# A second write of zeroes to the output, just ahead of the first store of a weighted sum

## Chip, cores, metric

One core of a Trainium2 chip. The metric is the device time of one execution in microseconds (us), as the median of several runs.

## What is computed

For each of 16 x 1024 tokens there are two expert outputs of 512 numbers and two weights; the result is their weighted sum, all in float32.

```python
weights = combine_weights[..., np.newaxis]          # (16, 1024, 2, 1)
return np.sum(expert_outputs * weights, axis=2)     # (16, 1024, 2, 512) -> (16, 1024, 512)
```

That is 67 MB to read, 34 MB to write and little arithmetic per byte.

## The kernel before

The 16,384 tokens are spread over the 128 partitions of the on-chip memory, 128 tokens to each partition. A partition's 128 tokens are cut into ten tiles of 12 or 13 tokens (`TILES`). The first nine tiles cover the first 128 x 115 rows of the arrays (`main` = 115 tokens a partition, with consecutive tokens of one partition lying together), the last tile the remaining 128 x 13 rows.

One large buffer `et` has four rooms (`ROOM`, 13, 13, 12 and 13 tokens). Tile g goes into room g mod 4. A load (line 76, `load`) brings the two expert outputs of a tile's tokens into its room, up to 53,248 bytes a partition. All loads are issued from SyncE's queue. The first five loads (`FIRST`: 2, 11, 13, 12 and 13 tokens; the first two make up tile 0) fill the four rooms; every later load is issued after the store that frees its room, and waits for that store's landing.

The sums (`combine`) are made in place. For tiles 0 to 7 VectorE multiplies the whole tile by the weights in one instruction (line 88) and adds the two halves in another (line 97); the sums land in the front part of the room. In tile 8 ScalarE does a part of the products (line 92); in tile 9 ScalarE makes one product and VectorE a fused multiply-add token by token (lines 102 and 103).

The stores (line 130) are issued from ScalarE's queue for tiles 0 to 6 and from SyncE's queue for tiles 7 and 8 (one store) and 9. Both queues feed the same 16 DMA engines.

The order of the instructions on each engine is that of the code (`tc.manual_schedule()`); waits between engines are set by the framework from what is read and written. Each DMA signals its landing on one of eight semaphore lanes, and a DMA that takes a lane over waits until the lane's last holder has landed. An additional DMA therefore shifts the lanes of those that come after it.

Before anything else VectorE sets the small tile `zt` (16 partitions of 128 numbers) to zero (line 108), and ScalarE's queue writes it to the output (line 111): with the first 128 x 115 rows of the output seen as 16 equal stretches (`ahead`), the first 512 bytes of each stretch become zero. The stores later put the true values there. After it, the same queue loads the weights (line 79: one load of 920 bytes a partition; line 114: two of 104 bytes for 64 partitions each).

Of the kernel before, what the change touches and what calls it, by code (L numbers as in the profile page):

```python
# [1 line left out]

# [4 lines left out]


@with_exitstack
def kernel(  # L10
    ctx: ExitStack,
    tc: tile.TileContext,
    expert_outputs: bass.AP,
    combine_weights: bass.AP,
    out: bass.AP,
):

    nc = tc.nc
    b, s, k, h = expert_outputs.shape
    assert k == 2
    n = b * s
    P = nc.NUM_PARTITIONS
    per = n // P
    assert per * P == n

    ROOM = [13, 13, 12, 13]
    ROOMS = len(ROOM)  # L30
    SITE = [sum(ROOM[:i]) for i in range(ROOMS)]
    TILES = [13, 13, 12, 13, 13, 13, 12, 13, 13, 13]
    FIRST = [2, 11, 13, 12, 13]
    STORES = [[0], [1], [2], [3], [4], [5], [6], [7, 8], [9]]
    WHOLE = [0, 1, 2, 3, 4, 5, 6, 7]
    MIXED = [8]
    ALONE = 3
    FREE = {9: 0}
    LAST = 13
    assert all(c <= ROOM[g % ROOMS] for g, c in enumerate(TILES))  # L40
    assert sum(TILES) == per and [g for st in STORES for g in st] == list(range(len(TILES)))
    main = per - LAST
    starts = [sum(TILES[:g]) for g in range(len(TILES))]

    def rows(x):

        first = x[0 : P * main, :].rearrange("(p t) f -> p t f", p=P)
        second = x[P * main : n, :].rearrange("(p t) f -> p t f", p=P)
        return lambda t, c: first[:, t : t + c, :] if t < main else second[:, t - main : t - main + c, :]

    flat = out.rearrange("b s h -> (b s) h")
    eo = rows(expert_outputs.rearrange("b s k h -> (b s) (k h)"))
    cw = rows(combine_weights.rearrange("b s k -> (b s) k"))
    o = rows(flat)

    dt = mybir.dt.float32
    mult = mybir.AluOpType.mult
    add = mybir.AluOpType.add
    copy = mybir.ActivationFunctionType.Copy

    pool = ctx.enter_context(tc.tile_pool(name="all", bufs=1))
    et = pool.tile([P, sum(ROOM), k * h], dt)
    halves = et.rearrange("p j (k h) -> p (j k) h", k=k)
    wt = pool.tile([P, per * k], dt)
    wk = wt.rearrange("p (t k) -> p t k", k=k)
    zt = pool.tile([16, 128], dt)
    warm = pool.tile([P, 1], dt)

    def place(t):
        g = max(g for g in range(len(TILES)) if starts[g] <= t)  # L70
        return SITE[g % ROOMS] + t - starts[g]

    def load(t, c, **kw):
        at = place(t)
        assert place(t + c - 1) == at + c - 1
        nc.sync.dma_start(out=et[:, at : at + c], in_=eo(t, c), **kw)  # L76

    def weights(q, t, c):
        q.dma_start(out=wk[:, t : t + c, :], in_=cw(t, c))

    def combine(g, base):
        at, c, t0 = SITE[g % ROOMS], TILES[g], starts[g]
        if g in WHOLE or g in MIXED:
            room = halves[:, k * at : k * (at + c), :]
            x0, x1 = et[:, at : at + c, 0:h], et[:, at : at + c, h : 2 * h]
            if g in WHOLE:
                wb = wt[:, k * t0 : k * (t0 + c)].unsqueeze(2).to_broadcast([P, k * c, h])
                nc.vector.tensor_tensor(out=room, in0=room, in1=wb, op=mult)  # L88
            else:
                for i in range(ALONE, c):  # L90
                    x = et[:, at + i, 0:h]
                    nc.scalar.activation(out=x, in_=x, func=copy, scale=wt[:, k * (t0 + i) : k * (t0 + i) + 1])  # L92
                w1 = wk[:, t0 : t0 + c, 1:2].to_broadcast([P, c, h])
                nc.vector.tensor_tensor(out=x1, in0=x1, in1=w1, op=mult)  # L94
                w0 = wk[:, t0 : t0 + ALONE, 0:1].to_broadcast([P, ALONE, h])
                nc.vector.tensor_tensor(out=x0[:, 0:ALONE], in0=x0[:, 0:ALONE], in1=w0, op=mult)  # L96
            nc.vector.tensor_tensor(out=halves[:, base : base + c, :], in0=x0, in1=x1, op=add)  # L97
            return
        for i in range(c):
            t = k * (t0 + i)  # L100
            x0, x1 = halves[:, k * (at + i), :], halves[:, k * (at + i) + 1, :]
            nc.scalar.activation(out=x0, in_=x0, func=copy, scale=wt[:, t : t + 1])  # L102
            nc.vector.scalar_tensor_tensor(  # L103
                out=halves[:, base + i, :], in0=x1, scalar=wt[:, t + 1 : t + 2], in1=x0, op0=mult, op1=add
            )

    with tc.manual_schedule():
        nc.vector.memset(zt, 0.0)  # L108

        ahead = flat[0 : P * main, :].rearrange("(q t) h -> q (t h)", q=16)  # L110
        nc.scalar.dma_start(out=ahead[:, 0:128], in_=zt)  # L111
        weights(nc.scalar, 0, main)
        for half in (slice(0, P // 2), slice(P // 2, P)):
            nc.scalar.dma_start(out=wk[half, main:per, :], in_=cw(main, per - main)[half])
        nc.scalar.activation(out=warm, in_=nc.const_aps.tensor(1.0, (P, 1), dt), func=copy)  # L115

        t = 0
        for i, c in enumerate(FIRST):
            load(t, c, **({"max_dma_last_dim": k * h * 4} if i == 0 else {}))
            t += c  # L120
        assert t == sum(TILES[:ROOMS])
        for j, st in enumerate(STORES):
            room = FREE.get(st[0], st[0] % ROOMS)
            base, c = SITE[room] * k, 0
            for g in st:
                combine(g, base + c)
                c += TILES[g]
            assert c <= k * ROOM[room]
            q = nc.sync if j in (7, 8) else nc.scalar
            q.dma_start(out=o(starts[st[0]], c), in_=halves[:, base : base + c, :])  # L130
            for g in st:
                if g + ROOMS < len(TILES):
                    load(starts[g + ROOMS], TILES[g + ROOMS])


# [1 line left out]
_INS = ['expert_outputs', 'combine_weights']  # L137
_OUTS = [((16, 1024, 512), 'float32')]


# [23 lines left out]
```

## Time and profile before

| | |
|---|---|
| median of 3 runs | 238.86 us (238.84 to 238.99) |
| profiled execution, first to last instruction (span) | 237.1 us; the page gives no other time of it |
| bytes moved | 100.80 MB, on average 425 GB/s |
| VectorE busy | 190.0 us |
| ScalarE busy | 15.8 us |

In the profile's rows DVE is VectorE, ACT ScalarE, SP SyncE, POOL GpSimd; a trailing q (ACTq, SPq) is the sequencer of that engine, which issues the DMAs. q1 is the DMA queue fed by SyncE, q10 that fed by ScalarE. `et`, `wt` and `zt` are the buffers named above, `out_dram` the output. L97 is line 97 of the kernel. In rows of DMA queues there stand packets, MB, and the time that the packets took as a share of 16 engines over the stretch asked for; a packet is counted where it begins, so that a short stretch can show over 100%.

### The profile page before, as it was taken

What the parts mean: (1) busy time and instruction counts of PE and PEld (TensorE: products, weight loads), DVE (VectorE), ACT (ScalarE), POOL (GpSimd) and SP (SyncE); (2) the same over time, 40 slices, a digit from 0 to 9 for tenths busy, and PEclk for the clock granted to TensorE, in tenths of its full rate; (3) what the DMA queues carried; (4) which work ended last, traced back from release to release, by engine and by line L of the source; (5) the groups of instructions that cost most, each with busy time, mean ns of one, the idle gap of its engine ahead of it and who ended that gap; (6) DMA issues with size and microseconds to landing.
All of it is one profiled execution on the core that took longest, in us unless ns stands there. A gap on an engine that the chain in (4) does not pass through costs nothing.

```text
span 237.1 us, 154 instructions
## 1 busy us (share of the span) xinstructions
DVE 190.0 (80%) x33; ACT 15.8 (7%) x25; POOL 0.2 (0%) x4
## 2 busy tenths in 40 slices
DVE  0006999999999999999999998998499969919400
ACT  2000000000000000000000000000000055019200
POOL 0000000000000000000000000000000000000000
DMA  8999999989999999999899999999899999899996
GB/s 300 388 481 434 432 421 398 470 348 485 449 431 458 431 440 390 486 420 420 359 492 409 409 509 392 431 503 431 359 431 503 420 397 483 381 431 431 431 431 287
DMA packets 3344, 100.80 MB, mean 425 GB/s; under 512 B 512, under 2 KB 656, under 8 KB 912
## 3 DMA queue, kind: packets, MB, share of 16 engines
q1 hardware_dynamic: 2000, 77.33, 75.9%
q10 hardware_dynamic: 1344, 23.47, 23.0%
HBM read 67.24 MB, written 33.56 MB: 425 GB/s over the span
## 4 chain that ended last, share of the span: by engine, by line
DVE 55%; DMA 36%; issue 1%; ACT 0%; DVEq 0%; ACTq 0%; SPq 0%
DVE et L88 35%; DVE et L97 17%; DMA out_dram<-et 17%; DMA et<-in_expert_outputs_dram 12%; DMA wt<-in_combine_weights_dram 8%; DVE et L103 3%; ACT et L102 0%; DVEq L159 0%; ACTq L111 0%; DVE zt L108 0%; DVEq L88 0%; SPq L76 0%; ACTq L102 0%
## 5 line engine op out<-in xcount | busy, mean ns | idle before, releaser
L88 DVE TENSOR_TENSOR et<-et,wt 128x13312 f32<-128x13312 f32 (+1 forms) x8 | 110.0, 13754 | 23.8 <-DMA wt<-in_combine_weights_dram 18.7
L97 DVE TENSOR_TENSOR et<-et 128x6656 f32<-128x6656 f32 (+1 forms) x9 | 62.8, 6973 | 0.4
L92 ACT ACTIVATE et<-et,wt 128x512 f32<-128x512 f32 x10 | 6.2, 708 | 188.0 <-DMA et<-in_expert_outputs_dram 188.0
L103 DVE SCALAR_TENSOR_TENSOR et<-et,wt 128x512 f32<-128x512 f32 x13 | 8.7, 747 | 5.0 <-ACT et L102 5.0
L102 ACT ACTIVATE et<-et,wt 128x512 f32<-128x512 f32 x13 | 8.1, 707 | 14.0 <-DMA et<-in_expert_outputs_dram 14.0
L94 DVE TENSOR_TENSOR et<-et,wt 128x6656 f32<-128x6656 f32 x1 | 7.1, 7093 | 2.3 <-DMA et<-in_expert_outputs_dram 2.3
L96 DVE TENSOR_TENSOR et<-et,wt 128x1536 f32<-128x1536 f32 x1 | 1.8, 1751 | 0.0
L115 ACT ACT_TABLE_LOAD x1 | 1.3, 1283 | 3.1 <-issue 3.1
L108 DVE MEMSET zt<- 16x128 f32 x1 | 0.2, 165 | 0.8 <-PEq L148 0.8
L115 ACT ACTIVATE warm<-const-float32-1.0 128x1 f32<-128x1 f32 x1 | 0.2, 203 | 0.0
L148 POOL MEMSET const-bfloat16-1.0<- 128x1 bf16 x1 | 0.1, 102 | 0.0
L148 POOL MEMSET const-uint8-127<- 128x1 uint8 x1 | 0.1, 101 | 0.0
L148 POOL MEMSET const-float32-0.0<- 128x1 f32 x1 | 0.1, 99 | 0.2 <-issue 0.2
L148 POOL MEMSET const-float32-1.0<- 128x1 f32 x1 | 0.1, 98 | 0.0
## 6 DMA issues: line engine op xcount, KB each, us to landing
et<-in_expert_outputs_dram SPq DMA_DIRECT2D x7, 6656.0 KB, 32.2
out_dram<-et ACTq DMA_DIRECT2D x5, 3328.0 KB, 34.7
et<-in_expert_outputs_dram SPq DMA_DIRECT2D x2, 6144.0 KB, 41.1
out_dram<-et SPq DMA_DIRECT2D x1, 6656.0 KB, 19.9
out_dram<-et ACTq DMA_DIRECT2D x2, 3072.0 KB, 37.2
et<-in_expert_outputs_dram SPq DMA_DIRECT2D x1, 5632.0 KB, 18.2
out_dram<-et SPq DMA_DIRECT2D x1, 3328.0 KB, 14.0
et<-in_expert_outputs_dram SPq DMA_DIRECT2D x1, 1024.0 KB, 5.0
```

What stands on the lines that cost most here:

```text
L88: nc.vector.tensor_tensor(out=room, in0=room, in1=wb, op=mult)
L92: nc.scalar.activation(out=x, in_=x, func=copy, scale=wt[:, k * (t0 + i) : k * (t0 + i) + 1])
L94: nc.vector.tensor_tensor(out=x1, in0=x1, in1=w1, op=mult)
L96: nc.vector.tensor_tensor(out=x0[:, 0:ALONE], in0=x0[:, 0:ALONE], in1=w0, op=mult)
L97: nc.vector.tensor_tensor(out=halves[:, base : base + c, :], in0=x0, in1=x1, op=add)
L102: nc.scalar.activation(out=x0, in_=x0, func=copy, scale=wt[:, t : t + 1])
L103: nc.vector.scalar_tensor_tensor(out=halves[:, base + i, :], in0=x1, scalar=wt[:, t + 1 : t + 2], in1=x0, op0=mult, op1=add)
L108: nc.vector.memset(zt, 0.0)
L115: nc.scalar.activation(out=warm, in_=nc.const_aps.tensor(1.0, (P, 1), dt), func=copy)
L148: nc = _bacc.Bacc("TRN2", target_bir_lowering=False, num_devices=1)
```

## The change

The write of zeroes, memset and DMA, becomes a function `touch`. It is called where the write stood, and a second time in `combine`, behind the product of tile 0 and ahead of its sum. So the second memset stands on VectorE between these two instructions, and the second DMA on ScalarE's queue ahead of the store of tile 0, which covers the same rows and is made to wait for it. Line numbers move by five to eight.

```diff
+    ahead = flat[0 : P * main, :].rearrange("(q t) h -> q (t h)", q=16)
+
+    def touch():
+        nc.vector.memset(zt, 0.0)
+        nc.scalar.dma_start(out=ahead[:, 0:128], in_=zt)
+
     def combine(g, base):
...
                 nc.vector.tensor_tensor(out=room, in0=room, in1=wb, op=mult)
+                if g == 0:
+                    touch()
             else:
...
     with tc.manual_schedule():
-        nc.vector.memset(zt, 0.0)
-
-        ahead = flat[0 : P * main, :].rearrange("(q t) h -> q (t h)", q=16)
-        nc.scalar.dma_start(out=ahead[:, 0:128], in_=zt)
+        touch()
         weights(nc.scalar, 0, main)
```

## The prediction

> **What bounds the kernel now.** I read the page first, for who is busy and how evenly.
>
> ```profile
> DVE 190.0 (80%) x33; ACT 15.8 (7%) x25; POOL 0.2 (0%) x4
> ...
> DMA  8999999989999999999899999999899999899996
> DMA packets 3344, 100.80 MB, mean 425 GB/s; under 512 B 512, under 2 KB 656, under 8 KB 912
> ```
>
> VectorE works for 80% of the span, yet the row of DMA tenths holds an 8 or a 9 in every slice but the last. The 16 DMA engines are the suspect. A mean can hide a stage in which they wait, so I cut the span into stages (columns: stretch, its length, busy time of each engine, clock, DMA share, GB/s).
>
> ```profile
> 0.00:20.00 20.00, 0.44 (x2) 1.49 (x2) 0.20 (x4) 1.00 0.95 390
> 20.00:62.00 42.00, 41.93 (x5) 0.00 (x0) 0.00 (x0) 1.00 0.99 424
> 62.00:110.00 48.00, 47.93 (x5) 0.00 (x0) 0.00 (x0) 1.00 1.02 439
> 110.00:145.00 35.00, 34.52 (x4) 0.00 (x0) 0.00 (x0) 1.00 0.99 430
> 145.00:208.00 63.00, 55.91 (x7) 6.23 (x10) 0.00 (x0) 1.00 1.00 431
> 208.00:237.00 29.00, 9.29 (x14) 8.07 (x13) 0.00 (x0) 1.00 0.95 411
> ```
>
> The DMA share is 0.99 to 1.02 in every stage but the first and the last (a packet is counted where it begins, hence the 1.02). From 20 to 145 us VectorE is full as well; after 145 it has gaps (55.91 of 63 us). So two resources are full in the middle, and only one of them stays full to the end. Who sets the end is read from the chain of waits and from the last stores.
>
> ```profile
> 144.62 39.25 DMA out_dram<-et
> 183.92 28.80 DMA et<-in_expert_outputs_dram
> 213.56 8.04 DVE et L103 x12
> ```
>
> ```profile
> out_dram<-et SPq DMA_DIRECT2D x1, 6656.0 KB, 19.9
> out_dram<-et SPq DMA_DIRECT2D x1, 3328.0 KB, 14.0
> ```
>
> ```profile
> 208.61 0.35 SPq L130 DMA_DIRECT2D out_dram<-et  x1
> 222.29 0.34 SPq L130 DMA_DIRECT2D out_dram<-et  x1
> ```
>
> The chain runs through a store, the last load and the last sums, but look at what the queue does meanwhile. The store of tiles 7 and 8 is issued at 208.61 and lands 19.9 us later, at 228.5. The last store is issued at 222.29, 6.2 us before that, stands behind it on the same queue and lands at 236.3. The engines thus always have a store waiting; a delay of the last load or of the last sums by some us would be swallowed by these 6.2 us. What sets the end is the amount of work of the DMA engines, not the chain. A change moves the time only if it gives each engine more or less to do, makes a packet last longer, or leaves all queues empty for a while.
>
> **The change part by part.** The compiled program of the changed kernel shows one more memset on VectorE between the first product and the first sum, one more small DMA on ScalarE's queue ahead of store 0, and shifted semaphore lanes. In the timeline the place is this:
>
> ```profile
> 0.81 0.17 DVE L108 MEMSET zt<- 16x128 f32 x1 [0.81 <-PEq L148]
> 1.01 0.39 ACTq L111 DMA_DIRECT2D out_dram<-zt  x1
> 1.22 1.62 SPq L76 DMA_DIRECT2D et<-in_expert_outputs_dram  x3
> 1.43 0.45 ACTq L79 DMA_DIRECT2D wt<-in_combine_weights_dram  x1
> 4.92 0.33 SPq L76 DMA_DIRECT2D et<-in_expert_outputs_dram  x1
> 19.73 14.02 DVE L88 TENSOR_TENSOR et<-et,wt 128x13312 f32<-128x13312 f32 x1 [18.75 <-DMA wt<-in_combine_weights_dram]
> 33.78 7.09 DVE L97 TENSOR_TENSOR et<-et 128x6656 f32<-128x6656 f32 x1
> 40.79 14.02 DVE L88 TENSOR_TENSOR et<-et,wt 128x13312 f32<-128x13312 f32 x1
> 40.91 0.34 ACTq L130 DMA_DIRECT2D out_dram<-et  x1
> ```
>
> The memset costs 0.17 us by its first instance, with a handover of about 0.03 us (product end 33.75, sum start 33.78). VectorE has no gap from 19.73 to 145, so stores 0 to 5 are issued about 0.2 us later. That is not on the path that sets the end: the queues hold other work, and the last store has its 6.2 us. Cost at the end: 0; with the cover gone it would be 0.2 us. The memset also waits until the first write of zeroes has read `zt`. That and the landings of the first DMAs stand here (KB each, us from issue to landing):
>
> ```profile
> et<-in_expert_outputs_dram SPq DMA_DIRECT2D x1, 6656.0 KB, 33.5
> et<-in_expert_outputs_dram SPq DMA_DIRECT2D x1, 1024.0 KB, 5.0
> wt<-in_combine_weights_dram ACTq DMA_DIRECT2D x1, 115.0 KB, 18.2
> wt<-in_combine_weights_dram ACTq DMA_DIRECT2D x2, 6.5 KB, 31.0
> out_dram<-zt ACTq DMA_DIRECT2D x1, 8.0 KB, 3.9
> ```
>
> The first zeroes were issued at 1.0 and landed 3.9 us later, at 4.9, almost 29 us before the second memset: no wait.
>
> The DMA itself adds 16 packets of 512 bytes and 16 completion packets. Their price is in the stretch from 4 to 5 us, where the first zeroes went out:
>
> ```profile
> q1 hardware_dynamic: 100, 0.41, 98.4%
> q10 hardware_dynamic: 32, 0.01, 3.6%
> ```
>
> These 32 packets took 3.6% of 16 engines for 1 us, 0.58 us of engine time in all or 0.036 us of each engine. Cost at the end: +0.036 us, since the engines are full. [...]
>
> Store 0 must now wait for the zeroes to land, since both write the same rows. The zeroes can be issued at about 34.0 us, store 0 at 41.1: a cover of 7.1 us, the first sum. Near end: they land after 3.9 us, as the first did. Far end: store 0's own first packets began in the window from 45.6 to 46.2 us, 4.8 us after its issue; behind them one more load packet may come ahead of the completion. The size of such a packet is in the windows from 38 to 39 us and from 43.4 to 44.4 us (16 packets of the load of tile 2 each):
>
> ```profile
> q1 hardware_dynamic: 16, 0.79, 181.5%
> ```
>
> ```profile
> q1 hardware_dynamic: 16, 0.79, 220.2%
> ```
>
> ```profile
> q10 hardware_dynamic: 16, 0.43, 164.5%
> ```
>
> (The last row is store 0's first round, from 45.6 to 46.2.) One load packet takes 1.815 us of its engine. So the far end is 34.0 + 4.8 + 1.8 and some tenths to be noticed, 41 us: store 0 starts on time, or late by at most one packet, 1.8 us. Behind it on ScalarE's queue stands store 1, which is not ready until 62. Who waits for store 0 is load 5, into the room it frees:
>
> ```profile
> 67.80 0.33 SPq L76 DMA_DIRECT2D et<-in_expert_outputs_dram  x1
> ```
>
> ```profile
> et<-in_expert_outputs_dram SPq DMA_DIRECT2D x1, 6656.0 KB, 71.7
> ```
>
> Load 5 was issued at 67.80. The load ahead of it, the fifth, was issued at 4.9 and landed 71.7 us later, at 76.6. The load queue therefore had 8.8 us of work left, and 1.8 us of delay disappear in it. Cost: 0.
>
> The lanes: in the program of before the fifth load waits for the first zeroes' lane. With one DMA more, the fourth load waits for the first load (landed 5.0 us after its issue, so before 7) and the fifth for the weights (landed 18.2 us after an issue at 1.4, at 19.6). The third load, issued between 1.2 and 2.2, keeps the queue occupied until about 35 (33.5 us). Both are queued 15 us before their turn: cost 0. Later lanes pair with transfers that landed long before.
>
> The term whose size I cannot read is what the zeroes do to the **first store's stall**. The load packets from 43.4 took 220.2% of a 1 us window over 16 packets, 2.202 us each against 1.815: each engine lost 0.387 us once, as its first output packet came up. Two ends: the zeroes take that stall away (-0.387 us), or they bring another of the same size (+0.387 us). The nearest row is that of the first zeroes themselves: around them (4 to 5 us) 100 load packets took 157 ns each, so 16 small writes stalled nothing visible there, and their having gone out did not spare store 0 its stall 39 us later. I take 0 and keep both ends.
>
> Sum: 0 (VectorE) + 0.036 (packets) + 0 (landing) + 0 (lanes) + 0 (stall) = +0.04 us on the profiled execution's span of 237.1 us. The page gives no time beyond the span; the median of the runs, 238.86, is 1.8 us above it, which I take as unchanged. Forecast: 238.9 us.
>
> **The rivals.** What a measurement of this kernel can tell from no change I put at 0.2%, 0.48 us.
>
> *First-store stall gone.* The second touch comes 5 to 7 us before store 0 instead of 37, and what was lost in between is still there. 238.86 + 0.036 - 0.387 = 238.5. For it speaks that the stall occurs at the first store only; against it, that I only guess that closeness in time matters. Still inside 0.48 us.
>
> *Second stall.* The zeroes meet full queues and 16 engines that are moving 49 KB packets, and stop them as store 0 did, while store 0's stall remains: 238.86 + 0.036 + 0.387 = 239.3. Inside 0.48 us, barely.
>
> *Slower: the zeroes find the path cold.* The dearest such thing in the trace is the start. In the first 4 us:
>
> ```profile
> q1 hardware_dynamic: 145, 0.59, 53.5%
> ```
>
> That is 236 ns a packet (0.535 x 64 us / 145), against the 157 ns from 4 to 5 us: 145 x 79 ns over 16 engines, 0.72 us lost on each engine. If the zeroes, standing between load packets around 38 us, cost that much, the time is 238.86 + 0.036 + 0.72 = 239.6. It is decided by the loss of each engine: from 0.44 us up the result is slower. Against it: store 0, the same direction in larger packets, cost 0.387.
>
> *The landing counts in full.* Store 0 waits one load packet longer and nothing takes it up: 238.86 + 1.8 = 240.7, if the load queue ran dry before load 5. Against it stand the 8.8 us above. [...]
>
> *VectorE decides.* Then the 0.2 us of memset show, 239.1; the gaps after 145 us speak against it, and it belongs to "same".
>
> **How the numbers follow.** Forecast as summed, with or without the 0.2 us of VectorE: 0.42. Stall gone: 0.18. Second stall: 0.11. These three are within 0.2%: 0.71. Cold path: 0.16; landing in full or another delay of its kind: 0.06; together slower, 0.22. Faster by over 0.48 us: no row offers it beyond the stall's 0.387; 0.07 for a first-store stall that is larger in unprofiled runs than in this one trace. The range takes in both ends of the stall and the cold path, 238.4 to 239.65; the landing and the larger gain, 0.13, stay outside.
>
> **What would show it.** In the changed profile: a memset of about 0.17 us between the first product and the first sum; the zeroes' landing under 7.1 us and store 0's issue at 41.1; the fifth load's issue near 19.7 with no dip of the DMA share between 30 and 80 us; load packets of 1.815 us around 36 to 42 (else a second stall), and 1.815 or 2.2 us at the packet ahead of store 0. The prediction is wrong if the DMA share falls anywhere between 20 and 232 us, or if packets elsewhere last longer than before.

## The result, and the profile after

The changed kernel took 239.16 us (median of 21 runs, 239.08 to 240.29) against 238.90 us (median of 21 runs, 238.81 to 239.09). The ratio is 1.0016, 95% interval 1.0010 to 1.0023: slower by some 0.16%, clear of noise but below the 0.2% that the prediction called no change. Three of the 21 executions took 240.06 to 240.29; the other 18 lie between 239.08 and 239.22. The ratio holds all of them, the medians differ by 0.26 us.

The page of the changed kernel, the rows that answer to those of before:

```profile
span 237.1 us, 158 instructions
...
DMA  7999999999989999999999999998999899999996
...
DMA packets 3376, 100.81 MB, mean 425 GB/s; under 512 B 528, under 2 KB 688, under 8 KB 944
```

There are 32 more packets, and the span is 237.1 us as before. That is the main thing to see: the profiled execution took 239.13 us, of which 237.1 are span, so about 2.0 us lie outside it. Each execution's time comes with its span (to 0.1 us); for the kernel before the difference is 1.77 to 1.78 us on average (81 executions), for the changed one 2.01 (21 executions). The typical loss of 0.25 us is in no line of the profile. The three long executions are another matter: their spans are 238.0 to 238.3 us.

The same stages as before, from the view by stretches:

```profile
0.00:20.00 20.00, 0.49 (x2) 1.49 (x2) 0.20 (x4) 1.00 0.94 390
20.00:62.00 42.00, 41.97 (x6) 0.00 (x0) 0.00 (x0) 1.00 1.02 434
62.00:110.00 48.00, 47.93 (x5) 0.00 (x0) 0.00 (x0) 1.00 0.99 426
110.00:145.00 35.00, 34.85 (x5) 0.00 (x0) 0.00 (x0) 1.00 1.02 440
145.00:208.00 63.00, 56.10 (x7) 6.23 (x10) 0.00 (x0) 1.00 0.99 429
208.00:237.00 29.00, 8.70 (x13) 8.07 (x13) 0.00 (x0) 1.00 0.95 411
```

The DMA share stays at 0.99 to 1.02 between 20 and 208 us. The place of the change, in the timeline (start, duration, engine, line):

```profile
5.70 0.33 SPq L76 DMA_DIRECT2D et<-in_expert_outputs_dram  x1
19.61 0.33 SPq L76 DMA_DIRECT2D et<-in_expert_outputs_dram  x1
19.67 14.03 DVE L94 TENSOR_TENSOR et<-et,wt 128x13312 f32<-128x13312 f32 x1 [18.70 <-DMA wt<-in_combine_weights_dram]
33.66 0.17 DVE L84 MEMSET zt<- 16x128 f32 x1
33.76 7.07 DVE L105 TENSOR_TENSOR et<-et 128x6656 f32<-128x6656 f32 x1
33.86 0.34 ACTq L85 DMA_DIRECT2D out_dram<-zt  x1
40.74 14.02 DVE L94 TENSOR_TENSOR et<-et,wt 128x13312 f32<-128x13312 f32 x1
42.38 0.35 ACTq L135 DMA_DIRECT2D out_dram<-et  x1
69.76 0.33 SPq L76 DMA_DIRECT2D et<-in_expert_outputs_dram  x1
```

The memset hardly delays the sum, which follows the start of the product by 14.09 us (19.67 to 33.76) instead of 14.05 (19.73 to 33.78). The zeroes are issued at 33.86 and store 0 at 42.38 instead of 40.91; load 5 follows at 69.76 instead of 67.80. Landing times, from the DMA view of the stretches in which these two were issued (the zeroes; the fifth load):

```profile
out_dram<-zt ACTq DMA_DIRECT2D x1, 8.0 KB, 8.4
```

```profile
et<-in_expert_outputs_dram SPq DMA_DIRECT2D x1, 6656.0 KB, 56.0
```

The fifth load, issued at 19.61, landed at 75.6; load 5 stood in the queue 5.8 us ahead of that. The packets around the zeroes, queue by queue: 37.8 to 38.8, 39.5 to 40.5, then the two load packets on either side of store 0's first, 45 to 46 and 48.2 to 49.2.

```profile
q1 hardware_dynamic: 16, 0.79, 181.5%
q10 hardware_dynamic: 12, 0.01, 2.0%
```

```profile
q1 hardware_dynamic: 16, 0.79, 181.5%
q10 hardware_dynamic: 16, 0.00, 1.4%
```

```profile
q1 hardware_dynamic: 16, 0.79, 213.2%
```

```profile
q1 hardware_dynamic: 16, 0.79, 200.6%
```

The load packets beside the zeroes take 1.815 us as ever: no second stall. Twelve engines wrote their zeroes around 38 us, four a load packet later. The stall of the first store is still there, in two pieces: 2.132 and 2.006 us instead of 1.815, so 0.317 + 0.191 = 0.51 us over the two packets. Before, the packet ahead of store 0's first had lost 0.387 us, and the one behind it, from 46.4 to 47.4, lost another 0.035:

```profile
q1 hardware_dynamic: 16, 0.79, 185.0%
```

That is 0.42 us over two packets before, and 0.09 us more in the change. In f3 below, which sends the same zeroes, the same two packets took 202.8% and 198.8% of 1 us, which is 0.213 + 0.173 = 0.39 us lost, so the 0.09 us are no steady cost of the zeroes.

### The profile page after: what moved, and what is told of

Read it like the earlier page. It is cut to its first block, busy times and chain, and to the rows that moved or that the text cites. A ratio compares the mean times of both kernels' runs of the same rounds, so it can differ in the third digit from the quotient of the medians.

```text
span 237.1 us, 158 instructions
## 1 busy us (share of the span) xinstructions
DVE 190.0 (80%) x34; ACT 15.8 (7%) x25; POOL 0.2 (0%) x4
## 4 chain that ended last, share of the span: by engine, by line
DVE 48%; DMA 36%; issue 8%; ACT 0%; DVEq 0%; ACTq 0%; SPq 0%
DVE et L94 29%; DMA out_dram<-et 17%; DVE et L105 16%; DMA et<-in_expert_outputs_dram 11%; DMA wt<-in_combine_weights_dram 8%; DVE et L111 3%; ACT et L110 0%; DVEq L164 0%; ACTq L85 0%; DVE zt L84 0%; DVEq L94 0%; SPq L76 0%; ACTq L110 0%
```

## The experiments

The letters A to G name theories; each is explained in the expectation in which it first stands. Instruction counts are those of each engine's compiled program, waits included (ScalarE, VectorE). "Outside" is time minus span, averaged over the executions; "long" counts executions with a span of 237.7 us or more. For the comparison, the kernel before beside these runs had 3 long ones in 81.

| kernel | ScalarE, VectorE | median us | outside us | long |
|---|---|---|---|---|
| before | 54, 49 | 238.86 to 238.88 | 1.77 to 1.78 | 3 of 81 |
| the change | 56, 51 | 239.16 | 2.01 | 3 of 21 |
| e1, memset only | 54, 51 | 238.88 | 1.80 | 0 of 11 |
| e2, DMA only | 55, 49 | 238.82 | 1.81 | 0 of 11 |
| e3, padding on both | 62, 57 | 239.32 | 2.22 | 0 of 11 |
| e4, both touches at the start | 56, 51 | 240.59 | 2.04 | 5 of 6 |
| e5, zeroes in tile 1's rows | 56, 51 | 239.10 | 2.01 | 0 of 11 |
| f1, padding on ScalarE | 56, 49 | 239.11 | 2.02 | 0 of 11 |
| f2, padding on VectorE | 54, 57 | 239.30 | 2.18 | 0 of 12 |
| f3, change without warm copy | 55, 51 | 238.89 | 1.78 | 2 of 12 |
| f4, touch behind the sum | 55, 50 | 240.00 | 1.78 | 5 of 5 |
| f5, zeroes 2 us later | 64, 51 | 239.41 | 1.79 | 4 of 11 |
| e6, no zeroes | 52, 48 | 239.50 | 1.78 | 4 of 5 |
| e8, second zeroes only | 54, 49 | 239.95 | 1.79 | 5 of 6 |

The first four ask whether the memset, the DMA or the mere length of the program costs the 0.25 us.

**Memset only.**

```diff
                 if g == 0:
-                    touch()
+                    nc.vector.memset(zt, 0.0)
```

> Only the second memset stays, the second DMA is left out. Theory A (the extra time lies outside the span, in fetching a longer program: the changed kernel fetched 7 blocks of 8192 bytes ahead of its first instruction, the one before 6): 239.16 us if 7 blocks are fetched, 238.90 if 6, and a span of 237.1 either way. Theory B (the zeroes' packets or their wait cost DMA time inside the span): 238.90. Theory C (one more DMA costs something at the program's ends, whatever it does): 238.90.

Ratio 1.0001 (0.9992 to 1.0010). The memset is free. This kernel fetched 6 instruction blocks and lies where all three theories put it.

**DMA only.**

```diff
                 if g == 0:
-                    touch()
+                    nc.scalar.dma_start(out=ahead[:, 0:128], in_=zt)
```

> Only the second DMA stays, the second memset is left out; the zeroes of the first are sent again, as early as the queue allows, and store 0 waits for them. Theory A: 239.16 with 7 instruction blocks, 238.90 with 6, span 237.1. Theory B: the zeroes go out in the first microseconds, away from store 0, so 238.9 and none of the executions about 1 us longer. Theory C: 239.16.

Ratio 1.0000 (0.9992 to 1.0009). Without the memset to wait for, the zeroes went out at 5 us (timeline):

```profile
5.19 0.34 ACTq L96 DMA_DIRECT2D out_dram<-zt  x1
40.95 0.35 ACTq L135 DMA_DIRECT2D out_dram<-et  x1
```

One more DMA costs nothing by itself, which ends theory C. What was fetched ahead of the first instruction (packets, MB, share) is this for this kernel and for the change:

```profile
q14 instruction: 14, 0.06, 1.2%
```

```profile
q14 instruction: 14, 0.06, 1.8%
```

Both fetched the same number of blocks, one more than before, and yet 1.81 us lie outside the span here and 2.01 in the change. That ends theory A in the form of block counts, and later runs agree: f1 fetched no more than the kernel before (13 packets) and has 2.02 us outside, f3 fetched the 14 of the change and has 1.78.

**Padding, no DMA.**

```diff
         nc.scalar.activation(out=warm, ...)
+        for _ in range(8):
+            nc.scalar.activation(out=warm, in_=nc.const_aps.tensor(1.0, (P, 1), dt), func=copy)
+            nc.vector.memset(spare, 0.0)
```

> The kernel before with eight more tiny ScalarE copies and eight more tiny VectorE memsets at the start, while both engines wait for data; no DMA is added. Theory A: 239.16 with 7 instruction blocks fetched, span 237.1, no executions about 1 us longer. Theories B and C: 238.90.

Ratio 1.0015 (1.0002 to 1.0028), span 237.1, and 2.22 us outside. Sixteen instructions that no one waits for cost somewhat more than the change: instructions alone can add time outside the span.

**Both touches at the start.**

```diff
+        touch()
         touch()
         weights(nc.scalar, 0, main)
...
-                if g == 0:
-                    touch()
```

> The same second memset and DMA as in the change, but directly behind the first ones. Theory A: 239.16 if 7 blocks are fetched, span 237.1. Theory B: 238.9 to 239.0 (the weights are queued some microseconds later), no executions about 1 us longer. Theory C: 239.16.

Ratio 1.0067 (1.0050 to 1.0084), which no theory had. 2.04 us are outside, and the rest is inside. The timeline and the queues from 72.3 to 77.3 us show how:

```profile
27.51 14.03 DVE L94 TENSOR_TENSOR et<-et,wt 128x13312 f32<-128x13312 f32 x1 [22.03 <-DMA wt<-in_combine_weights_dram]
```

```profile
73.66 0.33 SPq L76 DMA_DIRECT2D et<-in_expert_outputs_dram  x1
```

```profile
q10 hardware_dynamic: 96, 2.13, 99.1%
```

The weights, queued 4.4 us later behind the second zeroes, met large load packets and put the first product off from 19.73 to 27.51. Store 0 and load 5 came late, and from 72.3 to 77.3 no load packet was left: the load queue had run dry. The next four take the two effects apart.

**Zeroes in tile 1's rows, so that store 0 doesn't wait.**

```diff
-    def touch():
+    def touch(at=0):
         nc.vector.memset(zt, 0.0)
-        nc.scalar.dma_start(out=ahead[:, 0:128], in_=zt)
+        nc.scalar.dma_start(out=ahead[:, at : at + 128], in_=zt)
...
-                    touch()
+                    touch(TILES[0] * h)
```

The call at the start keeps `at` 0, so only the second zeroes move to tile 1's rows, and not both as the text on record has it.

> As the change, but both writes of zeroes go to rows of tile 1 (the same 16 stretches, 13 tokens further), so that store 1 and not store 0 waits for the second one. Theory D (the time is added outside the span, by the length of ScalarE's program: 54 and 55 instructions there gave 1.76 to 1.79 us outside the span, 56 gave 2.0, 62 gave 2.25): ScalarE has 56 here, so 239.1 with a span of 237.1. Theory B (waiting for the zeroes to land costs time): store 0 goes out at 41.0 and not 42.4, so 238.9. If the executions about 1 us longer come from store 0's late start, none are seen; if from the zeroes among the loads, about 1 in 7.

Ratio 1.0006 (0.9997 to 1.0015). Store 0 goes out on time:

```profile
40.87 0.35 ACTq L135 DMA_DIRECT2D out_dram<-et  x1
```

The interval of the ratio includes 1, but the 2.01 us outside, an average over 11 executions, remain without the wait, so the typical loss does not come from it. None of 11 executions is long.

**Padding on ScalarE.**

```diff
         nc.scalar.activation(out=warm, ...)
+        for _ in range(2):
+            nc.scalar.activation(out=warm, in_=nc.const_aps.tensor(1.0, (P, 1), dt), func=copy)
```

> The kernel before with two more tiny ScalarE copies at the start; no DMA and no VectorE instruction is added. Theory D: 56 instructions on ScalarE, so 239.1 with a span of 237.1, 2.0 us outside. Theory E (the length of all programs together, or of VectorE's, decides): two instructions more in all, fewer than the change's four, so 238.9 as with the memset alone, which also had two more.

Ratio 1.0008 (0.9999 to 1.0016), median up by 0.23 us. The interval just includes 1, as it takes in the two longest times of the kernel before, 239.28 and 239.80; all 11 times here (239.04 us or more) lie above 33 of the 35 there. It is the change's typical loss without any zeroes, from two instructions of 0.2 us at a time when ScalarE is idle.

**Padding on VectorE.**

```diff
         nc.scalar.activation(out=warm, ...)
+        for _ in range(8):
+            nc.vector.memset(spare, 0.0)
```

> The kernel before with eight more tiny VectorE memsets at the start; ScalarE's program stays as it was. Theory D: 238.88, 1.77 us outside a span of 237.1. Theory E: eight more in all, twice the change's, so 239.1 to 239.3.

Ratio 1.0015 (1.0007 to 1.0024), 2.18 us outside. VectorE's program can do it too, so theory D, ScalarE alone, was too narrow. Two more VectorE instructions (e1) cost nothing, eight cost 0.4 us. The steps do not add: with both paddings (e3) it is 2.22.

**The change without the warm copy.**

```diff
-        nc.scalar.activation(out=warm, in_=nc.const_aps.tensor(1.0, (P, 1), dt), func=copy)
```

> The change without the one tiny ScalarE copy at the start (its table load moves to the first product at about 192 us, 1.3 us where ScalarE has some 2.5 us to spare), which brings ScalarE's program from 56 to 55 instructions; the second write of zeroes stays. Theory D: 1.78 us outside a span of 237.1, so 238.9: the loss of the change is gone though its zeroes are not. Theory B: 239.1 to 239.2 as with the change.

This is the sharpest of them. The zeroes, the memset and the late store 0 are all there,

```profile
42.31 0.35 ACTq L134 DMA_DIRECT2D out_dram<-et  x1
```

and with ScalarE's program shorter by one instruction the median is 238.89 against 238.88, with 1.78 us outside. The ratio, 1.0004 (0.9992 to 1.0016), holds two long executions of 239.98 and 240.03: what takes the typical loss away does not take these away.

The last four ask what happens inside the span when store 0 is late.

**Touch behind the sum.**

```diff
-                if g == 0:
-                    touch()
...
             nc.vector.tensor_tensor(out=halves[:, base : base + c, :], in0=x0, in1=x1, op=add)
+            if g == 0:
+                touch()
```

> The second write of zeroes stands behind tile 0's sum instead of ahead of it, so nothing covers its landing: store 0 goes out at about 49 us, load 5 at about 76, when the load queue has run dry (its fifth load ended at 75.3 in the change). ScalarE has 55 instructions. Theory F (the executions about 1 us longer are those in which store 0 is so late that the load queue runs dry before load 5): a span of 238.0 to 239.0 in nearly all executions, 239.8 to 240.8 in all, and stretched load packets right after load 5's first. Theory G (store 0's lateness is harmless, only the time outside the span counts): span 237.1, 238.9.

Ratio 1.0047 (1.0035 to 1.0059), spans of 238.0 to 238.4 in all five. Store 0 went out at 47.92, load 5 at 73.66. From 72 to 77 us (first fence) only completions are left on the load queue; from 77 to 84 (second) loads start again. The third fence is the changed kernel from 77 to 84.

```profile
q10 hardware_dynamic: 100, 2.24, 104.1%
q1 hardware_dynamic: 8, 0.00, 0.1%
```

```profile
q1 hardware_dynamic: 32, 1.70, 67.0%
q10 hardware_dynamic: 36, 0.96, 33.1%
```

```profile
q1 hardware_dynamic: 32, 1.70, 56.2%
q10 hardware_dynamic: 44, 1.17, 38.8%
```

The engines stayed busy while the load queue was dry (104.1% in the first fence), so that alone cost nothing. But 32 packets at 67.0% of 16 engines over 7 us are 2.35 us each, against 1.97 in the change: each engine lost 2 x 0.38 = 0.76 us as loads joined the stores again. It resembles the first store's stall, with the directions exchanged. And the engines ended out of step. The DMA shares from 234 to 238 us in slices of 0.1 us, of the change and of this kernel (a packet stands where it begins, and the last ones take 0.99 us):

```profile
DMA  0000009999000000000000000000000000000000
```

```profile
DMA  6099696660669999606060600000000000000000
```

In the change all engines end within 0.4 us; here their ends, from the packet records, are spread over 1.0 us, and the last one counts.

**Zeroes two microseconds later.**

```diff
-                    touch()
+                    nc.vector.memset(zt, 0.0)
+                    for _ in range(8):
+                        nc.scalar.activation(out=late, in_=zt, func=copy)
+                    nc.scalar.dma_start(out=ahead[:, 0:128], in_=late)
```

> As the change, but eight tiny ScalarE copies of the zeroes stand between the second memset and the second DMA, so that the zeroes are issued about 2 us later and store 0 goes out at 44 to 46 us instead of 42.4. ScalarE has 64 instructions, so 2.25 us lie outside the span; it is the span that is looked at. Theory F: load 5 at 71.5 to 73.5, at the edge of the load queue's end: many more executions with 238.0 or more than the change's 3 in 21. Theory G: span 237.1 in all, 239.35.

Ratio 1.0020 (1.0011 to 1.0028). Neither theory holds. Load 5, at 72.09, came early enough: from 74 to 77 us the load queue went on with 32 packets, 0.85 MB. All 11 spans lie between 237.4 and 237.8, so the count of 4 in the table is the edge of one narrow group and not a second group. The one traced execution shows the larger part of the loss in the load packet ahead of store 0 (46.9 to 47.9 us):

```profile
q1 hardware_dynamic: 16, 0.79, 248.8%
```

That is 2.488 us, a stall of 0.67 us where the kernel before had 0.42 over its two packets: 0.25 us of the 0.4 by which this span is longer. And 64 ScalarE instructions left 1.79 us outside, not 2.25: the time outside does not simply grow with the length of a program.

**No zeroes at all.**

```diff
-        touch()
         weights(nc.scalar, 0, main)
...
-                if g == 0:
-                    touch()
```

> Neither write of zeroes. ScalarE has 52 instructions, VectorE 48. If zeroes sent in the first microseconds take something off the first store's stall, the load packet ahead of store 0 takes longer than 2.2 us (or more packets do) and the time is above 238.9; if they do nothing, the stall is 0.39 us again and the time 238.8 to 238.9. Time outside the span: 1.77 us, or 1.5 if shorter programs still save a step.

Ratio 1.0033 (1.0020 to 1.0046). Four of five executions have spans of 237.7 to 238.1. The trace that was taken is of the fifth, 237.0, and cannot say where the others lost their time. In it the load packets ahead of store 0 (43 to 45 us) show the usual stall:

```profile
q1 hardware_dynamic: 16, 0.79, 111.7%
```

That is 2.234 us each, 0.42 us lost, so in this execution the missing zeroes made it no larger. So the first write of zeroes is worth about 0.6 us at the median; whether by the first store's stall in the other four or by the order of the first transfers, which it also shifts, stays open.

**Only the second zeroes.**

```diff
-        touch()
         weights(nc.scalar, 0, main)
```

> Only the second write of zeroes, none at the start. ScalarE has 54 instructions, VectorE 49, so theory D expects 1.77 us outside the span and 238.9 as the usual time. If a first write of zeroes has to find its path, load packets around 38 us take longer than 1.815 us. Theory F: executions about 1 us longer, about 1 in 7, as store 0 waits for the zeroes until about 42.4.

Ratio 1.0042 (1.0028 to 1.0056): the second write doesn't replace the first. The outside time is as theory D said, 1.79. The load packets beside the only zeroes (38 to 40 us) and the end of the DMA work (234 to 238):

```profile
q1 hardware_dynamic: 19, 0.93, 107.8%
q10 hardware_dynamic: 19, 0.01, 1.3%
```

```profile
DMA  9009006699900900666900000000000000000000
```

19 load packets at 107.8% of 16 engines over 2 us are 1.816 us each: even without any zeroes before them, they hold up no load. A large part of the loss stands at the first store, issued at 42.07 (44 to 48.5 us):

```profile
q1 hardware_dynamic: 20, 0.98, 67.5%
```

That is 2.43 us for each of 20 load packets, 0.77 us for each engine, against 0.42 in the kernel before. The load queue did not run dry here: load 5 was issued at 69.87, and load packets still began between 73 and 77 us. The engines end out of step too, spread over about 1.1 us.

## Why the prediction was right, and where it was not

**The bound** held. The DMA share stayed full from 20 to 208 us, and the span did not move (237.1).

**The memset** cost 0 at the end, as said; even the 0.2 us of delay for VectorE did not appear, as from the first product's start to the second's are 21.07 us (19.67 to 40.74) instead of 21.06.

**The packets**, priced at 0.036 us, are too small to be told apart: no stretch shows them.

**The landing** took 8.4 us, more than the first zeroes' 3.9 us and more than the far end of the estimate, which had them landed by 41 us and not at 42.3: four engines served their zeroes a load packet later. So two of the signs named, a landing under 7.1 us and store 0 at 41.1, were not met; store 0 was 1.5 us late, within "at most one packet, 1.8 us". That store 0's wait cost the usual execution nothing is shown by f3. But the cover was overstated. The prediction gave load 5 a margin of 8.8 us; in the change 5.8 us were left, and not all of that can be used: in f4 a load issued at 73.66 left the queue dry until after 77.

**The lanes** behaved as read: the fourth and fifth loads were issued at 5.70 and 19.61, with no dip.

**The stall** was put at 0 between -0.39 and +0.39. The zeroes stalled nothing (1.815 us beside them in the change, 1.816 in e8), so second stall and cold path are ruled out; and they took nothing away. The first store's stall was 0.51 instead of 0.42 us over two packets. That the span came out level all the same was in part luck of that execution: its first 4 us moved 153 load packets instead of 145, which is 0.08 us of work for each engine at 157 ns a packet, and its first product began 0.06 us earlier.

```profile
q1 hardware_dynamic: 153, 0.63, 50.1%
```

This row also shows a flaw in the cold-path rival. By the sum that gave 0.72 us lost at the start, these 153 packets of 210 ns lost 0.50 us, 0.22 less, though only 0.08 us more work was done. The lengths of the packets at the start therefore do not measure the time lost there.

**The step that did not hold in the time** is the last of the sum: "the median of the runs, 238.86, is 1.8 us above it, which I take as unchanged". It grew to 2.01 us. The forecast of +0.04 us was right for the span of the usual execution and missed 0.25 us outside it, for which the prediction had no term. That the forecast still came so close rests on this term being small. f1 gets the same 0.25 us from two idle instructions, f3 is rid of it by one instruction less: the typical loss comes from the program's instructions and not from what the zeroes do. In the kernels with 56 instructions on ScalarE it is 2.01 to 2.04, in those with 52 to 55 (and VectorE at 48 to 51) 1.77 to 1.81; f2 and f5 show that no simple count of one engine explains it, and the number of instruction blocks fetched does not either (e2, f1, f3). What the chip does in that time is not seen in these traces.

**The long executions**, 3 of 21, lie above the range's end of 239.65 us and are not explained. With store 0 late by about 1.5 us (the change and f3) there are 5 in 33; in the kernels that keep the first zeroes and start store 0 on time (e1, e2, e3, e5, f1, f2) none in 67; before, 3 in 81, and none of the 21 above. That points to store 0's late start, but theory F, a dry load queue, is shown only for f4 and e4: in f5, later than the change, no span is above 237.8, and no trace caught a long execution of the change. The trace of e8, a long execution with store 0 at 42.07 and loads still queued, offers another candidate, a first-store stall of 0.77 us; whether the change's long executions have it is not shown.

## What to carry to other kernels

Before explaining a difference of a few tenths of a microsecond inside the profile, subtract the span from the time: here what lies outside changed with the instructions of the program, and a control with idle instructions told it from the effect of the edit. In a kernel bound by DMA a late store can cost nothing while both queues hold work, as in f3, but that is no guarantee: the first store's stall grew to 0.67 us in f5. Count the slack from the moment that a load must be issued, not from the moment that the queue runs dry. No version tried here beats the kernel before beyond its interval.

## What the runs showed of the hardware

- Where one direction joined the other after a stretch alone, each engine lost time over one or two packets: 0.42 us at the first store of the kernel before, 0.51 in the change, 0.39 in f3, 0.67 in f5, 0.77 in e8, and about 0.76 where loads rejoined stores in f4.
- Small writes between large loads did not slow them: 1.815 us a load packet beside the zeroes (the change) and without them (the kernel before).
- The same zeroes landed 4 us after issue at the start and 8.4 us beside full queues, as each engine served its share between load packets, twelve around 38 us and four a load packet later.
- Idle instructions alone changed the time by 0.23 to 0.46 us at an unchanged span of 237.1 us (f1, f2, e3).
